# Which projections run beside which attention, and latents that stay on the chip

## The chip, the cores and the metric

The kernel runs on one core of a Trainium2 chip. A core has a matrix engine (TensorE, PE in the profile; its weight loads are listed apart as PEld), VectorE (DVE), ScalarE (ACT), GpSimd (POOL) and SyncE (SP), whose queue issues nearly all transfers here; 16 DMA engines move the data. The metric is the device time of one execution in microseconds. All arithmetic is float32; a product is made of three passes over operands that are split into a high and a low part (`fp32r` in the profile).

## What is computed

The reference is an encoder of two layers over 1024 positions of 1024 features. In each layer one input projection feeds four groups of attention heads (A to D), whose outputs are joined, projected and added; an MLP follows. The change concerns the input projection and its consumers:

```
h = rms_norm(x, norm1_g[l])
proj = h @ w_in[l]
(a_cq, a_ckv, a_kr, b_q, b_k, b_v, c_q, c_k, c_v, d_q, d_k, d_v) = split(proj)
y_a = mla_mixer(a_cq, a_ckv, a_kr, ...)   # group A: latents
y_b = diff_mixer(b_q, b_k, b_v, ...)      # group B
y_c = swa_mixer(c_q, c_k, c_v, ...)       # group C: a window of 128
y_d = na_mixer(d_q, d_k, d_v, ...)        # group D: neighbours on a grid
```

and inside group A the second projections, which start from the latents:

```
q = (rms_norm(cq, q_norm_g) @ w_uq)       # cq: 192 wide; rope on 32 of each head's 96
c = rms_norm(ckv, kv_norm_g)              # ckv: 128 wide
k_nope, v = c @ w_uk, c @ w_uv
k_pe = apply_rope(kr)                     # 32 wide, shared by the heads
```

## The kernel before

Everything is held with features on the partitions and positions along the row. The input projection has 19 column tiles of 128. Each is 8 blocks of 128 x 128 weights against both halves (512 positions) of the normed x, three passes each: 48 matmuls. The normed x (`xs`, high and low) fills all 16 places of the pool of big tiles. The projection is taken on x times the gain, and the row factor of the norm (`rb`) is multiplied in when a tile is evacuated.

`attention` (line 377) goes through these stages in each layer. Two waves make the six tiles of group B. Then `weave` (line 541) interleaves a main stream with a fill stream: after each step of attention it takes some steps of a list of projections. Beside B's attention (`attn_b`, 18 steps) the fill is `proj_latent` (line 661, three tiles: cq, the rest of cq with the rotary key kr, and ckv) and then `proj_d` (six tiles). Beside D's attention (`attn_d`, line 1030, 36 steps) the fill is `proj_c` (four tiles) and then `latent_up` (line 692, the seven second projections of group A). Then come the attentions of C and A with parts of the output projection as fill, then the MLP. Small chains that finish the softmax and the norms (`tails`, advanced by `tick`) run in between.

The order of instructions on each engine is chosen by a planner when the program is built: it starts from the program's order and priorities (the main stream has an offset, `LB` 40 and `LD` 50) and a model of times. So fill work of B may still run when D begins. A tile of a pool waits until an earlier one of its tag is free.

The places that matter:

- `stack` (line 737): 8 places of 128 x 1024 (the pool that holds x between stages). A head of B takes four (two q, two k), one of D three, one of A four.
- big tiles: 16 places; `xs` until the last input projection, then `rq`, `rkv` (the two row factors of the latents' norms, spread over the partitions) and six `latp` (high and low of three latents), and later the mixed outputs.
- `part` (line 571): 3 places of 128 x 512 for an evacuated half; `both` (line 574): 2 places for its high and low.
- The rotary tables `tabc`, `tabs` (`table`, line 561): one place each. They are loaded and multiplied with the row factor: for B with `rb` on VectorE, for C with `rb` on GpSimd, for the latents' second projection with `rq` on GpSimd.

In `proj_latent` each half of a tile is evacuated (times `rb`, line 603), squared on ScalarE, summed over the partitions by four matmuls against ones (line 655), multiplied by the gain, split, and written to a DRAM tensor `lat` (`latent_parts`, line 647, and `emit_parts`, line 578). After the third tile two reciprocal roots (`rsqrt_cols`, line 241: eleven operations on eight columns) give the two row factors, which are transposed and written to DRAM (`rows_of`, line 266). `latent_up` spreads them over the partitions by a broadcasting load (`spread`, line 281), loads `lat` back into `latp`, the second tile of cq twice (64 rows, above and below, so that a product over 64 rows can take two weights at a time), and multiplies. The rope of a tile (`ev_rope`, line 586) is three VectorE operations, one addition on `self.eng` (GpSimd here), and the split, whose low part is also on GpSimd.

Of the kernel before, what the change touches and what calls it, by code (L numbers as in the profile page):

```python
# [98 lines left out]
def layout(i):  # L99
# [29 lines left out]
    gq = np.concatenate([i["mla_q_norm_g"], np.zeros((n, 64), np.float32)], 1)  # L129
# [16 lines left out]
class Trunk:  # L146
# [107 lines left out]
    def rstd_cols(self, sq, count, rhs, tag="mm"):  # L254
# [5 lines left out]
        for t in range(n):  # L260
            nc.tensor.matmul(ps[:, t * g:(t + 1) * g], sq[:, t * P:(t + 1) * P], rhs, start=True, stop=True)
# [115 lines left out]
    def attention(self, l):  # L377
# [11 lines left out]
        lat, krd = dr([2, 3, P, S], "lat"), dr([2, 16, 2, S], "krd")  # L389
# [30 lines left out]
        with ExitStack() as stack, ExitStack() as att:  # L420
            self.ap = att.enter_context(sbuf("att"))
            with self.banks(mm=2, tr=2, sb=3, pv=1):
                with sbuf("proj", "right") as self.pp:
# [32 lines left out]
                    fill = chain(self.proj_latent(l, one, xs, rb, tabs, lat, krd, rows), proj_d())  # L456
# [3 lines left out]
                    fill = chain(proj_c(), self.latent_up(l, lat, rows, qa, ka, va))  # L460
# [100 lines left out]
    def table(self, name, rb, eng):  # L561

        out = []
        for n in "cs":
            t = self.pp.tile([P, S], F, tag="tab" + n, bufs=1, name="tab" + n)
            self.load(t, self.d[n + name])
            self.tt(t, t, rb, eng=eng)
# [92 lines left out]

    def proj_latent(self, l, one, xs, rb, tabs, lat, krd, rows_out):
# [4 lines left out]
        for i, t, g in ((0, T_CQ, self.gq[:, l, 0:1]), (2, T_CKV, self.gkv[:, l:l + 1])):  # L666
            yield from one(t, xs, self.ev_plain(rb, lambda n, y: self.latent_parts(y, g, P, n, lat[:, i], squares[i])))
        c, s = tabs

        def ev(n, ps):  # L670
            sl = slice(n * 512, n * 512 + 512)
            y, t2 = self.part(), self.part()
            self.tt(y[0:64], ps[0:64], rb[0:64, sl])
            self.tt(y[64:112], ps[64:112], c[64:112, sl])
# [816 lines left out]
```

## Time and profile before

| What | Value |
|---|---|
| Three runs, median (lowest to highest) | 2729.45 us (2723.23 to 2731.46) |
| The profiled execution, time / span | 2728.97 / 2727.2 us |
| Mean granted TensorE clock | 0.967 |
| First softmax minimum of B (line 806), layer 0 / layer 1 | 88.1 / 1434.6 us |
| DMA traffic | 389.20 MB, mean 143 GB/s |

The profile is that of one execution. Views used below: the page (shares of each engine, the chain of work that ended last), the busy times of each engine in chosen stretches with the granted clock and the use of the DMA engines, the instructions in order of time with the idle time before each and what ended it, groups of instructions of one line and shape, and the list of transfers.

### The profile page before, as it was taken

What the parts mean: (1) busy time and instruction counts of PE and PEld (TensorE: products, weight loads), DVE (VectorE), ACT (ScalarE), POOL (GpSimd) and SP (SyncE); (2) the same over time, 40 slices, a digit from 0 to 9 for tenths busy, and PEclk for the clock granted to TensorE, in tenths of its full rate; (3) what the DMA queues carried; (4) which work ended last, traced back from release to release, by engine and by line L of the source; (5) the groups of instructions that cost most, each with busy time, mean ns of one, the idle gap of its engine ahead of it and who ended that gap; (6) DMA issues with size and microseconds to landing.
All of it is one profiled execution on the core that took longest, in us unless ns stands there. A gap on an engine that the chain in (4) does not pass through costs nothing.

```text
span 2727.2 us, 37613 instructions
## 1 busy us (share of the span) xinstructions
PE 2553.1 (94%) x12298; PEld 2110.1 (77%) x12298; DVE 1994.1 (73%) x3544; ACT 1430.9 (52%) x2547; POOL 1134.5 (42%) x754
## 2 busy tenths in 40 slices
PE   8989988899989999999999899889998999999997
PEld 6778876787778887888877688767886788878886
DVE  7787767674966669787567778677749666687786
ACT  4667757563534444444436676576635344444444
POOL 2555642111245554445435556331013455545552
PEclk9989999999989999999998899899999999999998
DMA  5534597231234447444244345972221444664431
GB/s 175 166 105 126 154 280 241 83 93 40 65 130 156 151 160 267 156 138 142 98 133 138 95 134 157 300 215 71 76 70 44 154 159 149 223 222 150 131 100 62
DMA packets 190516, 389.20 MB, mean 143 GB/s; under 512 B 23712, under 2 KB 30832, under 8 KB 190320
## 3 DMA queue, kind: packets, MB, share of 16 engines
q1 hardware_dynamic: 176496, 361.62, 43.0%
q10 hardware_dynamic: 13824, 25.17, 2.7%
q8 instruction: 98, 1.61, 0.3%
q14 instruction: 98, 0.80, 0.1%
HBM read 263.29 MB, written 123.41 MB: 142 GB/s over the span
## 4 chain that ended last, share of the span: by engine, by line
PE 70%; DVE 14%; DMA 7%; ACT 4%; issue 3%; SPq 1%; POOL 1%; DVEq 0%; ACTq 0%; POOLq 0%
PE u L220 8%; PE u L222 8%; PE u L221 8%; PE mm L220 5%; PE mm L221 5%; PE mm L222 5%; PE p L220 5%; PE p L221 5%; PE p L222 5%; PE sb L804 3%; PE tr L840 2%; DVE p L806 2%; DVE part L188 2%; PE pv L829 2%; PE pv L828 2%
## 5 line engine op out<-in xcount | busy, mean ns | idle before, releaser
L188 POOL TENSOR_TENSOR wl<-raw,wh 128x512 fp32r<-128x512 f32 x448 | 635.1, 1418 | 705.2 <-ACT wh L194 690.1
L194 ACT ACTIVATE wh<-raw 128x512 fp32r<-128x512 f32 x448 | 281.5, 629 | 579.8 <-PE u L221 315.0
L188 POOL TENSOR_TENSOR wl<-ws,wh 128x512 fp32r<-128x512 f32 (+1 forms) x112 | 148.1, 1325 | 456.9 <-ACT wh L194 426.0
L220 PE MATMUL u<-far,wh 128*128 128x512 f32 x768 | 301.5, 393 | 11.5 <-ACT ev L1237 8.3
L188 DVE TENSOR_TENSOR raw<-raw 128x512 f32<-128x512 f32 x256 | 226.4, 890 | 107.4 <-POOL wl L188 56.9
L222 PE MATMUL u<-far,wl 128*128 128x512 f32 x768 | 300.5, 391 | 1.9 <-POOL wl L188 1.9
L221 PE MATMUL u<-far,wh 128*128 128x512 f32 x768 | 300.3, 391 | 0.0
L188 DVE TENSOR_TENSOR ptl<-tr,pth 128x512 fp32r<-128x512 f32 (+2 forms) x384 | 238.3, 628 | 66.6 <-ACT pth L194 64.9
L809 ACT ACTIVATE p<-p,nm 128x1024 f32<-128x1024 f32 x192 | 220.1, 1147 | 99.8 <-DVE nm L806 98.9
L194 ACT ACTIVATE pth<-tr 128x512 fp32r<-128x512 f32 (+2 forms) x384 | 205.6, 546 | 121.0 <-PE tr L840 64.8
L220 PE MATMUL p<-far,wh 128*128 128x512 f32 x640 | 251.7, 393 | 7.6 <-DVE ev L188 7.6
L222 PE MATMUL p<-far,wl 128*128 128x512 f32 x640 | 250.9, 392 | 1.5 <-POOL wl L188 1.5
L221 PE MATMUL p<-far,wh 128*128 128x512 f32 x640 | 251.0, 392 | 0.0
L804 PE MATMUL sb<-stack 96*128 96x512 f32 x640 | 218.5, 424 | 24.7 <-DVE nm L806 24.0
L188 DVE TENSOR_TENSOR far<-act,far 128x512 fp32r<-128x512 f32 x224 | 208.6, 960 | 14.6 <-ACT far L194 14.6
L188 POOL TENSOR_TENSOR p<-p 128x1024 f32<-128x1024 f32 x64 | 154.3, 2415 | 141.1 <-ACT p L893 125.0
L220 PEld LDWEIGHTS u<-far,wh 128*128 128x128 f32 x768 | 145.4, 189 | 43.6 <-ACT ev L1237 9.2
L222 PEld LDWEIGHTS u<-far,wl 128*128 128x128 f32 x768 | 145.0, 189 | 33.2 <-POOL wl L188 2.7
L220 PE MATMUL mm<-xh,wh 128*128 128x512 f32 x416 | 169.4, 407 | 0.8 <-DVE rows L272 0.2
L806 DVE CUSTOM_DVE_ANT_0 p<-sb,zero,nm 128x512 f32<-128x512 f32 x192 | 142.4, 743 | 36.3 <-PE sb L804 32.8
L221 PEld LDWEIGHTS u<-far,wh 128*128 128x128 f32 x768 | 145.3, 189 | 30.2
L221 PE MATMUL mm<-xl,wh 128*128 128x512 f32 x416 | 166.6, 400 | 0.0
(243 smaller groups left out, 6147.0 us busy)
## 6 DMA issues: line engine op xcount, KB each, us to landing
act<-acts SPq DMA_DIRECT2D x224, 256.0 KB
raw<-in_w_up SPq DMA_DIRECT2D x128, 256.0 KB
acts<-ev SPq DMA_DIRECT2D x128, 256.0 KB
raw<-in_w_down SPq DMA_DIRECT2D x128, 256.0 KB
acts<-ev ACTq DMA_DIRECT2D x96, 256.0 KB
ws<-in_w_in SPq DMA_DIRECT2D x76, 256.0 KB
rz<-drows SPq DMA_DIRECT2D x40, 256.0 KB
stack<-kd SPq DMA_DIRECT2D x32, 256.0 KB
```

The costliest lines, as they stand in the source:

```text
L188: (eng or self.nc.vector).tensor_tensor(out=out, in0=a, in1=b, op=op)
L194: nc.scalar.activation(hi, src, AF.Copy)
L220: mm(ps, w[0], x[0][:, sl], start=start, stop=False)
L221: mm(ps, w[0], x[1][:, sl], start=False, stop=False)
L222: mm(ps, w[1], x[0][:, sl], start=False, stop=stop)
L804: self.nc.tensor.matmul(ps, q[:, qt * P:(qt + 1) * P], k[:, sl], start=i == 0, stop=i == len(passes) - 1)
L806: self.nc.vector.tensor_tensor_reduce(out=p[:, sl], in0=ps, in1=self.zero[:, 0:1].bitcast(F).broadcast_to([P, 512]), scale=-scale, scalar= ...
L809: self.nc.scalar.activation(p, p, AF.Exp, bias=nm[:, 1:2], scale=-1.0, accum_out=z)
L828: nc.tensor.matmul(out, v[:, kt], h[:, sl], start=kt == 0, stop=False)
L829: nc.tensor.matmul(out, v[:, kt], lo[:, sl], start=False, stop=kt == 7)
L840: nc.tensor.transpose(t[:, k * 256 + i * P:k * 256 + (i + 1) * P], p[:, (j * 2 + k) * P:(j * 2 + k + 1) * P], self.ident)
```

## The change

Beside B's attention now run `proj_d` and then `proj_c`; beside D's attention run `proj_latent` and then `latent_up`. The three latents are evacuated into float32 tiles of the `stack` kind, 128 x 1024, and stay there; after the third tile they are multiplied by the gain and split into `latp` without leaving the chip. `lat` in DRAM is gone. The second tile of cq is written twice, to partitions 0 to 63 and 64 to 127, so its squares count double and are weighted with 0.5, and its gain is doubled in the constants (a column of the same length). The rotary key is multiplied by `rb` first and then rotated with bare tables, which are loaded in `proj_latent`, kept, and multiplied with `rq` in `latent_up`. The reciprocal root of cq is issued before the third tile. `rstd_cols` writes its sums group by group, so that `spread` reads one contiguous row.

```
-    gq = np.concatenate([i["mla_q_norm_g"], np.zeros((n, 64), np.float32)], 1)
+    gq = np.concatenate([i["mla_q_norm_g"], i["mla_q_norm_g"][:, 128:192]], 1)
...
-            nc.tensor.matmul(ps[:, t * g:(t + 1) * g], sq[:, t * P:(t + 1) * P], rhs, start=True, stop=True)
+            nc.tensor.matmul(ps.rearrange("p (g t) -> p t g", g=g)[:, t], sq[:, t * P:(t + 1) * P], rhs,
+                             start=True, stop=True)
...
-        src = rows.rearrange("(t g) p -> g t p", g=g)[j]
-        n = dst.shape[0]
-        self.load(dst.rearrange("p (t q) -> p t q", t=8), src.partition_broadcast(n))
+        src = rows.rearrange("(g t) p -> g (t p)", g=g)[j]
+        self.load(dst, src.partition_broadcast(dst.shape[0]))
...
-                    fill = chain(self.proj_latent(l, one, xs, rb, tabs, lat, krd, rows), proj_d())
+                    fill = chain(proj_d(), proj_c())
                     self.weave(chain.from_iterable(self.attn_b(l, t, qb, kb, vb, y["b"]) for t in range(2)),
                                fill, self.RB, self.LB, every=self.EV[0])
                     self.tails.append(self.mix_b(mix, y["b"], self.gsub[:, l:l + 1]))
-                    fill = chain(proj_c(), self.latent_up(l, lat, rows, qa, ka, va))
+                    lat = []
+                    fill = chain(self.proj_latent(l, one, xs, rb, lat, krd, rows),
+                                 self.latent_up(l, lat, rows, qa, ka, va))
                     self.weave(self.attn_d(l, qd, kd, vd, y["d"]), fill, self.RD, self.LD, every=self.EV[1])
...
-    def latent_parts(self, y, g, rows, n, dst, squares):
+    def latent_squares(self, y, n, squares):
         nc = self.nc
-        sl = slice(n * 512, n * 512 + 512)
         sq = self.part()
-        nc.scalar.activation(sq[:rows], y[:rows], AF.Square)
+        nc.scalar.activation(sq, y, AF.Square)
         ps = self.bank("mm", [P, 4])
         for t in range(4):
-            nc.tensor.matmul(ps[:, t:t + 1], sq[:rows, t * P:(t + 1) * P], self.ones[:rows, 0:1],
-                             start=True, stop=True)
+            nc.tensor.matmul(ps[:, t:t + 1], sq[:, t * P:(t + 1) * P], self.ones[:, 0:1], start=True, stop=True)
         nc.vector.tensor_copy(squares[:, n * 4:n * 4 + 4], ps)
-        self.emit_parts(y[:rows], [(dst[:, :rows, sl].rearrange("a p s -> p a s"), slice(0, rows))],
-                        slice(0, rows), g[:rows])
...
+        y = [self.stack(F) for _ in range(3)]
+        c, s = self.tabs = self.table("32")
+
+        def plain(i):
+            def ev(n, ps):
+                sl = slice(n * 512, n * 512 + 512)
+                self.tt(y[i][:, sl], ps, rb[:, sl])
+                self.latent_squares(y[i][:, sl], n, squares[i])
+            return ev
...
+            for at in (0, 64):
+                self.tt(y[1][at:at + 64, sl], ps[0:64], rb[0:64, sl])
+            k, t, t2 = self.part(), self.part(), self.part()
+            self.tt(k[64:112], ps[64:112], rb[64:112, sl])
+            self.tt(t[64:112], k[64:112], c[64:112, sl])
+            self.tt(t2[64:80], k[96:112], s[96:112, sl])
+            self.tt(t2[96:112], k[64:80], s[64:80, sl])
+            self.tt(t[64:80], t[64:80], t2[64:80], ALU.add, self.eng)
+            self.tt(t[96:112], t[96:112], t2[96:112], ALU.subtract, self.eng)
...
+        yield from one(T_CQ, xs, plain(0))
+        yield from one(T_CQR, xs, ev)
+        q = squares[0]
+        nc.vector.scalar_tensor_tensor(out=q, in0=squares[1], scalar=0.5, in1=q, op0=ALU.mult, op1=ALU.add)
+        rms(q, 192)
+        yield from one(T_CKV, xs, plain(2))
+        rms(squares[2], 128)
+        for t, g in zip(y, (self.gq[:, l, 0:1], self.gq[:, l, 1:2], self.gkv[:, l:l + 1])):
+            h, lo = self.big_tile(R, "latp"), self.big_tile(R, "latp")
+            for sl in self.halves():
+                self.split(h[:, sl], lo[:, sl], t[:, sl], g)
+            lat.append((h, lo))
...
-        parts = []
-        for i, r in ((0, P), (1, 64), (2, P)):
-            p = []
-            for j in range(2):
-                t = self.big_tile(R, "latp")
-                for at in range(0, P, r):
-                    self.load(t.bitcast(F)[at:at + r], lat[j, i, :r])
-                p.append(t)
-            parts.append(tuple(p))
-        tabs = self.table("32", rq, nc.gpsimd)
+        for t in self.tabs:
+            self.tt(t, t, rq, eng=nc.gpsimd)
```

More of the change, by code (lines that the diff above doesn't have):

```diff
@@ L681, in ev, with rms @@
                 for h in range(2)], slice(64, 112))
[L682 to L687 removed]
+            self.latent_squares(y[1][:, sl], n, squares[1])
+        def rms(m, count):
             nc.vector.tensor_scalar(m, m, 1.0 / count, EPS, ALU.mult, ALU.add)
             rows_out.append(self.rows_of(self.rsqrt_cols(m)))
+        yield from one(T_CQ, xs, plain(0))
@@ L690, in proj_latent, with latent_up @@
         yield True
-    def latent_up(self, l, lat, rows, qa, ka, va):
+    def latent_up(self, l, parts, rows, qa, ka, va):
         nc, d = self.nc, self.d
@@ L724, in latent_up @@
         w0 = self.weights(d["w_lat"][l, 0])
-        yield from two([w0[0], both(w0[1])], parts[0:2], self.ev_rope(tabs, qr))
+        yield from two([w0[0], both(w0[1])], parts[0:2], self.ev_rope(self.tabs, qr))
         plain = lambda r, dst: self.ev_plain(r, self.to_parts(dst))
```

26 lines of the change are left out of this document (6 added, 20 removed).

## The prediction

> **What bounds the kernel now.** I read the page first, then the busy times by stretch, then the chain of waits and the instructions of the stretches that stood out.
>
> ```profile
> span 2727.2 us, 37613 instructions
> PE 2553.1 (94%) x12298; PEld 2110.1 (77%) x12298; DVE 1994.1 (73%) x3544; ACT 1430.9 (52%) x2547; POOL 1134.5 (42%) x754
> PE 70%; DVE 14%; DMA 7%; ACT 4%; issue 3%; SPq 1%; POOL 1%; DVEq 0%; ACTq 0%; POOLq 0%
> ```
>
> TensorE is the bound: 2553.1 of 2727.2 us, 70% of the chain that ended last. The change adds no product and takes none away, so it can win only idle TensorE time, or time in which TensorE ran below full clock. The next view is of stretches of the two attention layers; the columns are TensorE, weight loads, VectorE, ScalarE, GpSimd, each with its count, then the granted clock, the DMA share and GB/s.
>
> ```profile
> 150.00:190.00 40.00, 30.02 (x138) 23.74 (x137) 34.58 (x88) 24.54 (x38) 22.82 (x12) 0.79 0.29 80
> 190.00:340.00 150.00, 149.61 (x827) 127.90 (x826) 115.98 (x305) 112.28 (x182) 88.57 (x52) 1.00 0.48 136
> 340.00:420.00 80.00, 66.10 (x363) 55.78 (x361) 50.68 (x131) 45.32 (x114) 30.92 (x21) 0.94 0.99 284
> 360.00:390.00 30.00, 22.40 (x117) 19.43 (x117) 17.25 (x42) 13.82 (x33) 14.29 (x9) 0.89 1.02 294
> 390.00:500.00 110.00, 87.45 (x451) 67.51 (x450) 79.47 (x210) 70.74 (x179) 28.89 (x18) 0.91 0.70 217
> 1500.00:1540.00 40.00, 29.62 (x126) 22.05 (x125) 33.34 (x84) 23.26 (x37) 23.96 (x14) 0.74 0.28 80
> 1540.00:1690.00 150.00, 148.63 (x821) 125.53 (x820) 120.06 (x298) 109.14 (x175) 85.32 (x49) 1.00 0.45 129
> 1720.00:1740.00 20.00, 13.56 (x65) 11.74 (x64) 12.06 (x33) 8.22 (x21) 9.84 (x7) 0.83 1.04 282
> 1740.00:1850.00 110.00, 93.25 (x489) 75.68 (x488) 82.44 (x219) 73.86 (x186) 30.72 (x19) 0.91 0.76 227
> ```
>
> Three kinds of stretch repeat in both layers. At 150 and 1500, where the last of the three latent tiles is worked on beside group B, VectorE is at 34.58 of 40 us and TensorE loses 10 us and a fifth of its clock. From 190 and 1540 TensorE is full. From 340 to 420 the DMA engines are full (0.99), and TensorE loses time until about 500. I count a loss as idle time plus busy time times (1 - clock).
>
> What happens in the first kind, from the order in time of GpSimd, VectorE and TensorE:
>
> ```profile
> 165.72 2.33 POOL L188 TENSOR_TENSOR tabs<-tabs,rb 128x1024 f32<-128x1024 f32 x1
> 168.12 2.34 DVE L249 SCALAR_TENSOR_TENSOR rs_t<-rs_r 128x8 f32<-128x8 f32 x2
> 173.63 0.80 PE L804 MATMUL sb<-stack 96*128 96x512 f32 x1 [4.98 <-DVE nm L806]
> 174.92 0.23 DVE L249 SCALAR_TENSOR_TENSOR rs_t<-rs_r 128x8 f32<-128x8 f32 x2
> ```
>
> The two reciprocal roots of `proj_latent` (line 689) are chains of eight-column operations. Two of them take 0.23 us at 174.92 but 2.34 us at 168.12, while GpSimd multiplies group C's rotary table and a softmax tile. The softmax minimum (line 806) queues behind them, and TensorE waits 4.98 us for it. In the second kind the chain of waits runs through transfers:
>
> ```profile
> 358.15 7.51 DMA rkv<-drows
> 365.69 11.75 DMA latp<-lat
> 399.02 5.40 DMA bias<-in_bias
> 404.43 9.07 DMA stack<-kc
> 413.57 9.20 DMA kan<-both
> 1713.22 10.30 DMA latp<-lat
> 1723.60 11.52 DMA stack<-kd
> ```
>
> `latent_up` needs eight free big tiles, and the normed x holds all sixteen until the last input projection; only then are scales and latents read back, 19.3 us in layer 0.
>
> **The change part by part.** *Order of the thirteen tiles beside B and D.* Each is 48 matmuls.
>
> ```profile
> 357.53 0.40 PE L222 MATMUL mm<-xh,wl 128*128 128x512 f32 x1
> ...
> 360.95 0.39 PE L222 MATMUL mm<-xh,wl 128*128 128x512 f32 x1
> ...
> 363.36 0.39 PE L222 MATMUL mm<-xh,wl 128*128 128x512 f32 x1
> ```
>
> Between the first two starts lie fifteen steps (the third is the last of the thirteen tiles): 3.42 / 15 = 0.228 us, so a tile costs 10.9 us of TensorE. B's fill gets one tile more (six of D and four of C for three latent and six), D's one less: plus 10.9 us where TensorE is full and minus 10.9 us later, in each layer. I cost this at **0**: up to the end of the thirteenth tile it is the same work in another order, and proj_c already overlaps B's end: its stores and B's last transposes (line 840) stand side by side.
>
> ```profile
> 313.80 13.16 SPq L167 DMA_DIRECT2D qc<-both  x6
> 353.51 0.44 PE tr L840 x4
> 424.64 0.39 DVE p L1084
> ```
>
> If D's start gives nothing back, it costs up to 2 x 10.9 = 21.9 us.
>
> *The burst at B's start.* It leaves with `proj_latent`, and proj_d's evacuations, simpler, come first. Loss now: 9.98 + 30.02 x 0.21 = 16.3 us in layer 0, 10.38 + 29.62 x 0.26 = 18.1 us in layer 1; together 34.4. The reciprocal roots and evacuations do not vanish; they go to D's start, where VectorE has 150 - 115.98 = 34 us of spare time, but the softmax behind them is as exposed. They no longer stand beside the multiplication by group C's table, though the one for `rq` may take its place. Between 0 and -34.4 I take half: **-17**.
>
> The Trainium skill's page "TensorE: Matmul & The Clock Gate" (Part 1: The HAM clock gate) says the clock halves after an idle window of about 3.4 us and returns after a busy one. The 4.98 us gap and the clock of 0.79 agree in kind; by the page one gap per layer would give back an estimated 1.7 us of clock, and the half would be about -12 instead of -17.
>
> *Latents on the chip.* What no longer moves, from the list of DMA issues:
>
> ```profile
> lat<-both SPq DMA_DIRECT2D x8, 512.0 KB
> latp<-lat SPq DMA_DIRECT2D x8, 512.0 KB
> kc<-both SPq DMA_DIRECT2D x8, 256.0 KB
> vc<-both SPq DMA_DIRECT2D x4, 512.0 KB
> latp<-lat SPq DMA_DIRECT2D x8, 256.0 KB
> lat<-both SPq DMA_DIRECT2D x4, 256.0 KB
> ```
>
> Per layer 4 x 512 + 4 x 256 KB = 3 MB of loads go, and 2.5 MB of stores. SP issues 14 DMAs fewer per layer. The loss at the read-back is 7.60 + 22.40 x 0.11 = 10.1 us in layer 0 and 6.44 + 13.56 x 0.17 = 8.7 in layer 1. The scales `rq` and `rkv` still go through DRAM (7.51 us) and still wait for big tiles; of the wait only 11.75 of 19.26 us is the latents': 0.61 x 18.8 = **-11.5**, between 0 and -18.8. The new hand-over, a split from SBUF straight into the freed tiles, has the same six halves as the old `emit_parts`, at another time.
>
> *Less traffic in the full stretch.* From 340 to 420 us some 284 GB/s x 80 us = 22.7 MB move. The 3 MB of latents and the 2 MB of kc and vc, which now go out beside B, are 22% of that. Ahead of group C the chain waits 23.7 us for bias, kc and kan. The losses from 390 to 500 and from 1740 to 1850 hold 22.55 + 16.75 = 39.3 us of idleness; 22% of it is **-8.6**, between 0 and twice that.
>
> *Added VectorE work.* `proj_latent` writes the half tile of cq twice and multiplies k by rb first.
>
> ```profile
> L188 DVE TENSOR_TENSOR part<-mm,rb 128x512 f32<-128x512 f32 x12 | 8.2, 686 | 0.8 <-PE mm L222 0.8
> L198 DVE SCALAR_TENSOR_TENSOR both<-part,par,both 128x512 fp32r<-128x512 f32 x8 | 8.7, 1092 | 1.2 <-ACT both L197 1.2
> ```
>
> That is two operations more per half, 2 x 2 x 2 x 0.686 = 5.5 us in all; VectorE's spare time covers most: **+2** of 0 to 5.5.
>
> *Places.* Three latents in float32 take three of the eight `stack` places until they are split. A head of D takes three, so one head's last keys can't be fetched until its forerunner is done. Such a load stood 11.52 us on the chain at 1723.60. Two heads per layer could be hit: 0 to 46 us. Some 33 us of latent tiles cover TensorE meanwhile, so I take **+5**. If that cover is used up, the whole wait shows, and the late thing next is C's first head, whose loads stand behind D's on SP's queue.
>
> *Nothing:* the contiguous spread, the group-first order of `rstd_cols`, the doubled gain and the factor 0.5 change forms, not counts; they are hidden under TensorE's full stretches, and uncovered they are below one eight-column operation each.
>
> Sum: -17 - 11.5 - 8.6 + 2 + 5 = -30 us. The profiled execution took 2728.97 us around its span of 2727.2, against a median of 2729.45: forecast **2699 us**, 2674 to 2716 if this case holds.
>
> **The rivals.** *All of it* (chance 0.10): burst and latents' losses vanish whole: -34.4 - 18.8 - 8.6 + 2 = -60, 2669 us. For it: both losses stand in both layers. Against: the reciprocal roots remain.
>
> *The burst only moves* (0.16): at D's start it costs what it cost at B's. -11.5 - 8.6 + 2 + 5 = -13, 2716 us. For it: the work is the same and VectorE stays in order.
>
> *GpSimd beside B* (0.12). The evacuations of C's rotary tiles put two GpSimd operations on each of six halves per layer next to B's softmax.
>
> ```profile
> L188 POOL TENSOR_TENSOR both<-part,both 128x512 fp32r<-128x512 f32 x48 | 64.8, 1354 | 60.3 <-ACT both L194 51.8 <-DMA ws<-in_w_out 4.1 <-PE mm L270 2.7
> L188 POOL TENSOR_TENSOR part<-part 128x512 f32<-128x512 f32 x24 | 32.9, 1369 | 20.7 <-DVE part L188 17.7 <-PE tr L221 1.3 <-PE tr L222 1.3
> ```
>
> Six times (1.354 + 1.369) is 16.3 us a layer, 33 in all. If each held up a VectorE operation for its whole length and TensorE with it, the gain of about 30 would be eaten: 2729 us, no change. Against it: such operations already run near 340 us with TensorE full, and VectorE at 115.98 + 16.3 of 150 would still fit. The Trainium skill's page "SBUF — State Buffer" (SBUF: two separate sides) has the rule behind this: VectorE with two SBUF inputs and GpSimd take one shared port pair in turn, and the loser blocks for the whole instruction. The 2.34 against 0.23 us above agrees.
>
> *The places decide* (0.22), on the other side: the three latents hold the `stack` places, D's heads run one after another behind their loads, and D's end, not TensorE, sets when C and A start. From the point where the wait is longer than the 33 us of latent tiles it shows in full: +46 + 5.5 - 17 - 11.5 = +23, 2752 us. For it: the pool was full with two heads of B, and D's loads are on the chain. Against: the latents are split right behind the last tile.
>
> *It doesn't do what it says* is kept inside these: if the planner spread proj_c past B's end as it does now, the latents would come after 363 us with their roots uncovered, which is the burst rival or worse.
>
> **How the numbers follow.** The forecast has 0.40. Runs before spread over 8 us, 0.3%, which is about what can be told from no change here. Faster by more: 0.40 + 0.10 + most of the burst rival, 0.62. Within: the GpSimd rival, 0.12. Slower: places and the worse ends, 0.26. The range runs from the full gain, 2667, to short of the places' price, 2746, which leaves out some 0.06 below and 0.13 above.
>
> **What would show it.** The slice at B's start (150 to 190) should have TensorE near 1.00 clock and no wait over 2 us behind line 806; the latents' names gone from the chain; the idle stretch after the last input tile shorter than 7.6 us; the stretch to C's end with less than 22 us idle. Wrong would be: reciprocal roots of 2 us and TensorE waiting behind them at D's start, `stack<-kd` on the chain for tens of us, C's first scores (line 1084, here 424.64 us) later than before. The prediction as a whole is wrong if TensorE's idle time in attention doesn't fall.

## The result, and the profile after

| Kernel | Median | Against before (95% interval) | Span of the profiled execution |
|---|---|---|---|
| before | 2729.83 us | | 2727.2 us |
| after | 2760.14 us (2759.86 to 2761.17, 4 runs) | 1.0116 (1.0099 to 1.0134) | 2758.0 us |

The change makes the kernel about 31 us slower; 2699 was forecast, with 2746 as the upper end. Of the experiments below, scales_ready and fill_faster each had one execution of four that was far longer (4800.74 and 7433.23 us), which is left out of their medians and ratios. Head of the page after:

```profile
span 2758.0 us, 37539 instructions
PE 2569.0 (93%) x12298; PEld 2119.4 (77%) x12298; DVE 1996.7 (72%) x3552; ACT 1432.7 (52%) x2547; POOL 1138.7 (41%) x754
```

The products are the same 12298, but they took 2569.0 us in place of 2553.1, at a mean granted clock of 0.962 in place of 0.967, and there is more idleness besides. To see where, each attention layer is cut into five stretches at points of its own trace: from B's first score 100 us on, then to the last input projection (377.5 us in layer 0 of after), to the last second projection, to the end of C's softmax, and to the end of A's scores. First the kernel before, with the columns as in the prediction (stretch, its length, TensorE, weight loads, VectorE, ScalarE, GpSimd, clock, DMA share, GB/s):

```profile
83.00:183.00 100.00, 84.81 (x406) 68.30 (x405) 85.47 (x203) 68.25 (x110) 57.76 (x33) 0.86 0.46 134
183.00:363.00 180.00, 179.38 (x993) 153.46 (x993) 132.11 (x347) 128.97 (x220) 98.48 (x57) 1.00 0.53 149
363.00:438.00 75.00, 59.11 (x322) 48.74 (x321) 55.91 (x141) 47.01 (x121) 25.98 (x17) 0.93 0.95 287
438.00:479.00 41.00, 34.55 (x182) 26.39 (x182) 29.67 (x94) 29.00 (x78) 9.78 (x6) 0.92 0.65 199
479.00:624.00 145.00, 132.72 (x788) 112.51 (x787) 107.19 (x241) 87.63 (x154) 21.53 (x12) 0.96 0.27 81
1431.00:1531.00 100.00, 84.93 (x390) 67.42 (x389) 82.23 (x195) 65.20 (x104) 56.62 (x32) 0.81 0.44 127
1531.00:1717.00 186.00, 184.40 (x1010) 156.15 (x1009) 139.86 (x354) 130.67 (x225) 98.81 (x59) 1.00 0.51 146
1717.00:1786.00 69.00, 55.90 (x298) 47.08 (x297) 50.78 (x129) 42.47 (x105) 25.40 (x17) 0.88 0.99 295
1786.00:1840.00 54.00, 44.56 (x229) 35.54 (x229) 40.37 (x115) 37.31 (x96) 18.16 (x10) 0.91 0.67 195
1840.00:1969.00 129.00, 123.26 (x761) 106.09 (x760) 98.36 (x230) 83.27 (x150) 12.81 (x8) 1.00 0.27 79
```

And the same view of the kernel after:

```profile
85.00:185.00 100.00, 90.31 (x443) 73.77 (x443) 71.52 (x174) 65.26 (x104) 56.09 (x31) 0.93 0.47 147
185.00:377.00 192.00, 180.49 (x975) 152.25 (x974) 147.62 (x366) 133.39 (x224) 101.00 (x59) 0.95 0.40 112
377.50:450.00 72.50, 55.68 (x254) 44.79 (x253) 50.93 (x134) 38.72 (x99) 24.64 (x16) 0.79 0.87 250
450.00:513.00 63.00, 51.03 (x262) 40.73 (x261) 43.58 (x125) 40.78 (x105) 18.12 (x10) 0.89 0.60 173
513.00:641.00 128.00, 122.17 (x750) 104.63 (x749) 97.54 (x228) 82.36 (x147) 12.81 (x8) 1.00 0.29 80
1447.00:1547.00 100.00, 92.99 (x464) 76.27 (x463) 75.40 (x180) 66.48 (x106) 54.34 (x31) 0.95 0.46 145
1547.00:1736.00 189.00, 177.29 (x958) 148.62 (x957) 144.97 (x360) 130.97 (x221) 100.79 (x59) 0.96 0.41 112
1736.00:1808.00 72.00, 53.85 (x253) 41.96 (x252) 48.39 (x132) 38.52 (x98) 25.00 (x17) 0.81 0.89 250
1808.00:1874.00 66.00, 53.65 (x262) 41.14 (x262) 46.53 (x126) 41.58 (x106) 18.13 (x10) 0.87 0.56 168
1874.00:2001.00 127.00, 121.87 (x753) 105.04 (x751) 97.60 (x226) 82.30 (x147) 12.80 (x8) 1.00 0.28 80
```

The loss of a row is its idle time plus busy time times (1 - clock), as in the prediction. The first row of before gives 15.19 + 84.81 x 0.14 = 27.1 us, that of after 9.69 + 90.31 x 0.07 = 16.0. The table adds both layers and takes the last two stretches together; four of the experiments below stand beside them, worked out alike:

| Loss of TensorE, both layers, us | before | after | order_only | copy_scalar | light_all | one_copy |
|---|---|---|---|---|---|---|
| first 100 us of B | 58.3 | 27.7 | 26.0 | 24.0 | 25.5 | 47.4 |
| then to the last input projection | 2.2 | 39.3 | 38.6 | 36.9 | 25.0 | 8.8 |
| then to the last second projection | 39.8 | 56.9 | 82.2 | 51.1 | 39.2 | 36.5 |
| then to the end of A's scores | 46.0 | 47.9 | 44.6 | 39.8 | 40.0 | 40.7 |
| sum | 146.3 | 171.8 | 191.5 | 151.8 | 129.7 | 133.4 |
| sum against before | | +25.5 | +45.2 | +5.5 | -16.6 | -12.9 |
| span against before | | +30.8 | +49.9 | +3.8 | -16.2 | -13.0 |

The last two lines agree within 5.3 us in every column, so the time is in these stretches. The burst at B's start did shrink, by 30.6 us, but 37.1 us came back by the end of the input projection, and another 17.1 by the end of the second projections. Idle time alone rose from 95.4 to 110.2 us over the ten stretches; the prediction had named idle time that doesn't fall as the sign that it is wrong as a whole.

What took its place stands at D's start. VectorE in order of time there, and the ten microseconds around it, in the kernel after:

```profile
380.00:390.00 10.00, 5.99 (x40) 4.98 (x38) 9.83 (x30) 6.63 (x21) 4.70 (x2) 0.97 1.04 279
```

```profile
380.74 0.73 DVE L198 SCALAR_TENSOR_TENSOR latp<-stack,par,latp 128x512 fp32r<-128x512 f32 x1
...
383.93 2.10 DVE L249 SCALAR_TENSOR_TENSOR rs_t<-rs_r 128x8 f32<-128x8 f32 x1
...
386.43 1.94 DVE L188 TENSOR_TENSOR rs_t<-rs_t,sq 128x8 f32<-128x8 f32 x1
...
389.40 0.17 DVE L188 TENSOR_TENSOR rs_t<-rs_t,sq 128x8 f32<-128x8 f32 x1
```

VectorE makes the low parts of the latents, a head's softmax and a reciprocal root in the same ten microseconds, one after another: it is busy for 9.83 of them, TensorE for 5.99. Two eight-column steps take 2.10 and 1.94 us where the same kind takes 0.17 a little later. GpSimd does at that time what the prediction named as a possible successor, the products of the rotary tables with `rq`:

```profile
383.64 2.37 POOL L188 TENSOR_TENSOR tabc<-tabc,rq 128x1024 f32<-128x1024 f32 x1 [3.91 <-DMA rq<-drows]
385.97 2.37 POOL L188 TENSOR_TENSOR tabs<-tabs,rq 128x1024 f32<-128x1024 f32 x1
```

The Trainium skill's page "SBUF — State Buffer" (SBUF: two separate sides) has a VectorE operation with two SBUF inputs and a GpSimd operation take a shared port pair in turn. These two pairs agree with it, as the pair of before did: each VectorE step ends within 0.03 us of the GpSimd product beside it.

TensorE's own order shows how far the second projections have moved away from the last input projection, after:

```profile
377.54 0.39 PE L222 MATMUL mm<-xh,wl 128*128 128x512 f32 x1
391.49 0.78 PE L220 MATMUL mm<-latp,wh 128*128 128x512 f32 x1
```

and before, where 363.36 us was the last input projection:

```profile
366.98 0.50 PE L220 MATMUL mm<-latp,wh 128*128 128x512 f32 x1 [1.33 <-DMA latp<-lat]
```

From the last input tile to the first second projection it is 14 us instead of 3.6; in between TensorE works on D's heads and stands idle for 4.4 us. Later, in group C, ScalarE and VectorE in order of time after:

```profile
427.72 0.51 ACT L1097 ACTIVATE p<-p,nb 128x256 f32<-128x256 f32 x1 [1.45 <-DVE nb L1094]
...
435.13 0.60 ACT L645 ACTIVATE both<-mm 128x512 fp32r<-128x512 f32 x1 [5.59 <-DMA kan<-both]
...
445.89 0.61 DVE L1094 CUSTOM_DVE_ANT_0 p<-sb,mask,nsink 128x384 f32<-128x384 f32 x1
...
448.00 0.61 ACT L1097 ACTIVATE p<-p,nb 128x384 f32<-128x384 f32 x1
```

The second projections' results wait for one of the two `both` places to be stored, and C's softmax stands behind them: it started at 427.72, its next minimum on VectorE (line 1094) comes at 445.89 and its next exponential on ScalarE (line 1097) at 448.00, some 20 us later.

### The profile page after: what moved, and what is told of

It reads as the page before. It is cut to its first block, busy times and chain, and to the rows that moved or that the text cites. A ratio compares the mean times of both kernels' runs of the same rounds, so it can differ in the third digit from the quotient of the medians.

```text
span 2758.0 us, 37539 instructions
## 1 busy us (share of the span) xinstructions
PE 2569.0 (93%) x12298; PEld 2119.4 (77%) x12298; DVE 1996.7 (72%) x3552; ACT 1432.7 (52%) x2547; POOL 1138.7 (41%) x754
## 2 busy tenths in 40 slices
DMA packets 182386, 377.64 MB, mean 137 GB/s; under 512 B 23264, under 2 KB 26288, under 8 KB 182192
## 4 chain that ended last, share of the span: by engine, by line
PE 68%; DVE 14%; DMA 6%; ACT 4%; issue 4%; POOL 2%; SPq 0%; DVEq 0%; ACTq 0%; POOLq 0%
PE u L220 8%; PE u L222 8%; PE u L221 7%; PE p L220 5%; PE p L221 5%; PE p L222 5%; PE mm L220 5%; PE mm L221 5%; PE mm L222 4%; PE sb L814 3%; DVE p L816 3%; DVE part L188 2%; PE tr L850 2%; DVE ptl L188 1%; PE pv L839 1%
## 5 line engine op out<-in xcount | busy, mean ns | idle before, releaser
L814 PE MATMUL sb<-stack 96*128 96x512 f32 x640 | 215.7, 418 | 13.1 <-DVE nm L816 12.2
L850 PE MATMUL tr<-ident,p 128*128 128x128 f32 x1024 | 159.9, 275 | 9.9 <-DVE ptl L188 6.0
```

The source lines that it names most:

```text
L814: self.nc.tensor.matmul(ps, q[:, qt * P:(qt + 1) * P], k[:, sl], start=i == 0, stop=i == len(passes) - 1)
L850: nc.tensor.transpose(t[:, k * 256 + i * P:k * 256 + (i + 1) * P], p[:, (j * 2 + k) * P:(j * 2 + k + 1) * P], self.ident)
```

## The experiments

Ratios are to the kernel before on the same chip, whose median in these batches was 2726 to 2731 us. Theories: the order is what costs (latents last, their chain in the open); the `stack` places hold up D; VectorE's work at D's start is too much; the scales or the form of the spread.

**order_only.** The new order, with the latents still through DRAM and without the double write of the query's half tile (after to this):

```
+            self.emit_parts(y, [(lat[:, i, :r, sl].rearrange("a p s -> p a s"), slice(0, r))], slice(0, r),
+                            gains[i][:r])
...
-            for at in (0, 64):
-                self.tt(y[1][at:at + 64, sl], ps[0:64], rb[0:64, sl])
+            self.tt(k[0:64], ps[0:64], rb[0:64, sl])
...
+                    self.load(t.bitcast(F)[at:at + r], lat[j, i, :r])
```

> The changed order of the projections, but the latents go through DRAM as before (no latent holds a stack place; the cq tile isn't written twice, so two VectorE operations per half of that tile are gone as well). Theory P (places: the three latents in the stack pool delay the loads of D's second head): about the time before, 2715 to 2735 us, and D's second head scores within 10 us of the first. Theory O (order: the latents' evacuations, squares and roots beside D's start, and latent_up later, cost the time wherever the latents lie): about the time after, 2750 to 2765 us, with TensorE idle around the last latent tile.

Measured: 2776.59 us, 1.0170 (1.0148 to 1.0193), beyond both ranges. Of the two VectorE operations that the expectation counts as gone, the edit takes out one, the second write. When the latents pass through DRAM the order costs 46 us (the key's multiplication ahead of its rotation and the shared tables are in it too). The stretch from the last input projection to the last second one in each layer, and of layer 0 the chain of waits:

```profile
380.00:456.00 76.00, 49.31 (x236) 38.23 (x235) 45.97 (x112) 33.13 (x78) 25.52 (x17) 0.80 0.81 236
1751.00:1832.00 81.00, 51.98 (x206) 37.08 (x206) 45.55 (x100) 30.02 (x68) 25.17 (x17) 0.68 0.73 209
```

```profile
388.25 7.64 DMA bias<-in_bias
...
405.03 8.53 DMA latp<-lat
413.69 0.78 PE mm L741
```

The latents now come last, so their way out to DRAM and back is open: TensorE loses 82.2 us there, against 39.8 before. D's first two heads start at 336 and 354 us, as early as before (337 and 355), so this loss is not in D's places.

**places_held.** Before, with three `stack` tiles written before proj_c and read after it:

```
+                        held = [self.stack(F) for _ in range(3)]
+                        for t in held:
+                            nc.gpsimd.memset(t[:, 0:2], 0.0)
                         yield from proj_c()
+                        for t in held:
+                            nc.scalar.activation(t[:, 0:2], t[:, 0:2], AF.Copy)
```

> The kernel before, with three stack places taken from the start of D's fill until group C's projections are done (three small writes, three small reads). Theory P: 2750 to 2765 us, D's second head late by 20 to 30 us as in the changed kernel. Theory O: the time before, 2722 to 2738 us.

Measured: 2727.65 us, 0.9997 (0.9985 to 1.0009). It proves nothing, since the reads stand far ahead of proj_c's end in the planner's order. GpSimd's first write of a place, and ScalarE's read of it:

```profile
270.66 0.10 POOL L463 MEMSET stack<- 128x2 f32 x1
```

```profile
272.35 0.19 ACT L466 ACTIVATE stack<-stack 128x2 f32<-128x2 f32 x1
```

**d_first** and **spread_only.** Before, with D's projections ahead of the latents beside B, and before with only the new form of the spread:

```
-  fill = chain(self.proj_latent(l, one, xs, rb, tabs, lat, krd, rows), proj_d())
+  fill = chain(proj_d(), self.proj_latent(l, one, xs, rb, tabs, lat, krd, rows))
```

> The kernel before with the fill beside B turned round: D's projections first, then the latents' (still before group C's, still through DRAM). Theory P says nothing of it but no loss: 2715 to 2735 us. Theory O: the burst of latent work moves from B's start to the middle of B, where TensorE has B's whole stream beside it, and latent_up isn't delayed: 2710 to 2730 us. If the burst costs the same wherever it stands, 2727 to 2733.

> The kernel before with the contiguous spread and the group-first order of the sums alone. Both theories: no change that can be told, 2722 to 2735 us.

Measured: 2725.68 us, 0.9989 (0.9978 to 1.0001), and 2729.45 us, 1.0000 (0.9988 to 1.0012). Neither is a cause. With D first the latents leave B's start without a gain in time, which is what "the burst only moves" says. The first two stretches of layer 0 in d_first:

```profile
83.00:183.00 100.00, 98.09 (x506) 81.69 (x505) 78.61 (x195) 72.35 (x117) 55.53 (x33) 1.00 0.50 157
183.00:363.00 180.00, 165.33 (x909) 139.22 (x908) 142.61 (x363) 127.58 (x219) 100.64 (x57) 0.93 0.49 135
```

They lose 1.9 and 26.2 us, where before lost 27.1 and 0.6: the whole burst came back in the next stretch, without D's start or the new hand-over.

**scales_ready** and **fill_faster.** After, with the two row factors read from input tables that are there from the start (so the right scaling is left out); and after with a denser fill beside D (the ratio of steps to fill 1 to 2 rather than 3 to 2):

```
-        self.spread(rq, rows[0])
+        self.load(rq, d["c32"])
```

```
-    NP, RB, RD, LB, LD = 6, (7, 8), (3, 2), 40, 50
+    NP, RB, RD, LB, LD = 6, (7, 8), (1, 2), 40, 50
```

> The changed kernel with the two row factors of the latents' norms replaced by loads of input tables, which wait for no root (so group A's second projections are scaled wrongly; the roots and their transposes are still computed). If the chain root, transpose, DRAM, spread at the end of the latents is what delays latent_up and C: 2735 to 2748 us, the stretch from the last input tile to the last second projection shorter by 8 to 12 us in each layer. If the cost is the latents' evacuation beside D's start and the late end of the input tiles: 2752 to 2762 us.

> The changed kernel with two fill steps for each step of D instead of two for three: the latents come ahead of D's first heads in the program. If the loss is in the pace of the fill (latents and second projections too late for C): 2735 to 2750 us. If the latents' evacuation costs TensorE time wherever it stands at D's start: 2755 to 2770 us.

Measured: 2761.71 us, 1.0125 (1.0107 to 1.0142): the chain of scales isn't waited for. And 2792.63 us, 1.0239 (1.0222 to 1.0256), beyond both ranges: a denser fill beside D is worse. What it runs short of, the run doesn't show.

**one_copy** and **one_copy_d_first.** Before's order; each latent goes to DRAM once in float32, comes back into three `stack` places at the head of D's fill, and is split on the chip behind proj_c. The second has D's projections ahead of the latents:

```
-        self.emit_parts(y[:rows], [(dst[:, :rows, sl].rearrange("a p s -> p a s"), slice(0, rows))],
-                        slice(0, rows), g[:rows])
+        self.keep(dst[:rows, sl], y[:rows])
...
+                        y = [self.stack(F) for _ in range(3)]
...
+                                self.load(y[i][at:at + r], lat[i, :r])
+                        yield from proj_c()
...
+                                self.split(h[:, sl], lo[:, sl], t[:, sl], g)
```

> The order of the kernel before; the latents go through DRAM as one float32 copy, are loaded into three stack places at the start of D's fill and split on the chip once big tiles are free. If the part of the change that keeps latents out of the read-back is good in itself and only the order is bad: 2708 to 2722 us, with no wait for latents after the last input tile. If the read-back of the kernel before was hidden anyway: 2724 to 2734 us.

> The same with D's projections ahead of the latents' beside B: the sum of the two if they add, 2704 to 2720 us; no better than the one before if the loss at B's start only moves, 2708 to 2724.

Measured: 2716.69 us, 0.9963 (0.9950 to 0.9975), faster than both kernels; and 2728.99 us, 1.0007 (0.9992 to 1.0021), slower than either expectation: D's projections first cost 12 us here and nothing in d_first, and no run says why. In the table, one_copy gains most in the first 100 us of B (47.4 for 58.3), where the latents' splits no longer stand, and only 3.3 us up to the last second projection. In one_copy three places are in fact held while D begins, from the loads to the splits:

```profile
329.05 2.29 SPq L160 DMA_DIRECT2D stack<-lat  x3
```

```profile
354.81 0.71 ACT L197 ACTIVATE latp<-stack,par 128x512 fp32r<-128x512 f32 x1
```

D's first head starts at 336 us all the same, and the second at 356 (before 355). That the latents hold places is thus not enough to make the kernel slower.

**fill_slower.** After, with a thinner fill beside D:

```
-    NP, RB, RD, LB, LD = 6, (7, 8), (3, 2), 40, 50
+    NP, RB, RD, LB, LD = 6, (7, 8), (2, 1), 40, 50
```

> The changed kernel with one number altered: beside group D's heads the fill is drawn two parts to one step of attention instead of three to two. If the time is lost only because latents and second projections are drawn at the wrong pace (faster was 34 us worse), 2735 to 2745 us. If the loss is the latents' own chain at D's start (evacuation, squares, split, each in VectorE's order), the pace is no remedy: 2755 us or more. The share of the second projections' end in the loss should be seen in the time of the last latp matmul, 450.0 us in the changed kernel.

Measured: 2742.42 us, 1.0047 (1.0027 to 1.0068), some 19 us better than after and in the range given for the pace. But the last second projection still ends at 449.1 us (450.0), so the gain isn't that the second projections end earlier; C's softmax ends at 500 instead of 513.

**light_evac** and **light_all.** After, with lighter work for the latents; both make the first edit and leave out the row factor and the rotation of the key; light_all also makes the second, leaves out the roots and reads the row factors from tables:

```
-            for at in (0, 64):
-                self.tt(y[1][at:at + 64, sl], ps[0:64], rb[0:64, sl])
+            self.tt(y[1][0:64, sl], ps[0:64], rb[0:64, sl])
+            nc.scalar.activation(y[1][64:128, sl], y[1][0:64, sl], AF.Copy)
```

```
-                self.split(h[:, sl], lo[:, sl], t[:, sl], g)
+                nc.scalar.activation(h[:, sl], t[:, sl], AF.Copy, scale=g)
+                nc.scalar.activation(lo[:, sl], t[:, sl], AF.Copy, scale=g)
```

> The changed kernel with a lighter evacuation of the second latent tile: the rotation of the rotary key is left out (that key is wrong), and the upper copy of the query's half tile is made by ScalarE from the lower one, so per half four VectorE operations of about 0.7 us and two of GpSimd go, 8 and 4 in a layer. If VectorE's load at D's start sets the loss in proportion, 8 x 0.69 x 2 layers = 11 us come back: about 2749. If the loss is where the latents stand and not what they cost VectorE, 2757 to 2762, with the last input tile still about 14 us later than in the kernel before.

> As light_evac, and in addition the reciprocal roots with their row transposes are left out (scales come ready from input tables, so all scaling by them is wrong), and the low parts of the latents are made by a second ScalarE copy instead of VectorE's subtraction (the low part is wrong). Some 16 VectorE operations of a half tile and both chains of roots go in a layer. If VectorE's work for the latents at D's start is the cost, nearly the whole loss goes: 2725 to 2740. If it is that the second projections begin only when the last input tile is done and split, however light the work, it stays within 10 us of the changed kernel: 2750 to 2762. Between the two, both have a share, and the difference to light_evac is the share of roots and splits.

Measured: 2731.71 us, 1.0005 (0.9990 to 1.0020), and 2708.85 us, 0.9926 (0.9901 to 0.9950). Both beat what was expected of them: the operations taken out return more than their own time. In light_all the first second projection follows the last input one by 6 us, and the stretch of the second projections loses no more than before (39.2 us in both layers, 39.8 before).

**added_off, split_off, roots_off, better.** They part the gain of the last two: after without the two operations per half that the change adds (the first edit of light_evac and the one here); with the splits of light_all alone; without the roots alone (row factors from tables); and with relief by other engines (copy by ScalarE, low part by GpSimd, thinner fill).

```
-            self.tt(k[64:112], ps[64:112], rb[64:112, sl])
-            self.tt(t[64:112], k[64:112], c[64:112, sl])
+            self.tt(t[64:112], ps[64:112], c[64:112, sl])
```

```
-            rows_out.append(self.rows_of(self.rsqrt_cols(m)))
+            pass
```

```
-                self.split(h[:, sl], lo[:, sl], t[:, sl], g)
+                nc.scalar.activation(t[:, sl], t[:, sl], AF.Copy, scale=g)
+                self.split(h[:, sl], lo[:, sl], t[:, sl], None, nc.gpsimd)
```

> The changed kernel without the two operations per half that the change adds: the upper copy of the query's half tile is made by ScalarE, and the rotary key isn't multiplied by its row scale (left out, so the key is wrong); the rotation itself stays. Four VectorE operations of 0.69 us per layer go, 5.5 us of VectorE time in all. light_evac, which leaves out the rotation too (two more VectorE and two GpSimd operations per half), was 28 us faster than the changed kernel. If the added work is the larger part of it, 2738 to 2746; if the moved rotation with its GpSimd steps is, 2751 to 2758. By the prediction's own term, +2, it would be 2758.

> The changed kernel with the low parts of the latents made by a second ScalarE copy instead of VectorE's subtraction (the low part is wrong, the rest stands): six VectorE operations of 0.86 us per layer go, 10 us in all, of those between the last input tile and the second projections. light_all was 23 us faster than light_evac, by roots and splits together. If the split is the larger part, 2740 to 2748 here and roots_off above 2753; if the roots are, the other way round.

> The changed kernel with both reciprocal roots and their row transposes left out, and their scales read from input tables (all scaling by them is wrong): some 17 small VectorE operations each go from D's start, and the second projections no longer depend on them. scales_ready, which kept the roots but did not wait for them, was as slow as the changed kernel, so a gain here would be VectorE's time and not the wait: 2738 to 2748 if the roots are the larger part of the 23 us, above 2753 if the split is.

> Nothing is left out: the changed kernel with VectorE relieved where another engine can do the step, the upper copy of the query's half tile by ScalarE, the low part of each latent by GpSimd (which needs the gain applied by ScalarE first), and the fill beside D at two parts to one step. The slower fill alone gave 18 us, light_evac 28. If VectorE's load at D's start is the cause, 2720 to 2735, near the kernel before or under it. If GpSimd's longer subtraction (about 1.4 to 2 us a half) only takes the place of VectorE's in the chain from the last input tile to the second projections, 2735 to 2745, no better than the slower fill alone.

| | Median | Ratio (95%) |
|---|---|---|
| added_off | 2731.79 us | 1.0020 (1.0008 to 1.0031) |
| split_off | 2746.66 us | 1.0075 (1.0055 to 1.0096) |
| roots_off | 2746.38 us | 1.0070 (1.0054 to 1.0087) |
| better | 2741.42 us | 1.0052 (1.0037 to 1.0066) |

Against after's 1.0116 the added work is worth 0.96%, 26 us, the splits and the roots 11 and 13 us, about half each, which neither expectation had. With light_evac's 1.11% the three make 1.98%, near light_all's 1.90%, so these three gains add. In better they don't: it is no better than the thinner fill alone.

**copy_scalar, mended, mended_slower.** After with only the upper copy of the half tile moved to ScalarE (the diff under light_evac); with the key's multiplication by `rb` taken off VectorE too, by tables multiplied on GpSimd and loaded again for the second projections; and this with the thinner fill.

```
-        c, s = self.tabs = self.table("32")
+        c, s = self.table("32", rb, nc.gpsimd)
...
-        for t in self.tabs:
-            self.tt(t, t, rq, eng=nc.gpsimd)
+        tabs = self.table("32", rq, nc.gpsimd)
```

> Nothing is left out: the changed kernel with the upper copy of the query's half tile made by ScalarE; the key's multiplication by its row scale stays on VectorE. added_off, without both added steps, gave back 28 us. If the double write is the larger part, 2732 to 2742; if the key's multiplication, which stands ahead of the rotation and takes a third scratch tile, is, 2750 to 2760.

> Nothing is left out: both added steps taken off VectorE. ScalarE makes the upper copy, and the rotary tables are multiplied by the row scale on GpSimd and loaded again for the second projections, as in the kernel before. If added_off showed the price of the added VectorE work and not of the missing key scale, 2728 to 2738. If GpSimd's two table products (2.3 us each beside D's softmax) and the second loading cost what they cost beside B, 2740 or more.

> As mended, with the fill beside D at two parts to one step. If the slower fill's 18 us and the added work's 28 us are separate losses, 2710 to 2722, under the kernel before. If both act through the same thing, VectorE's load per us at D's start, 2725 to 2738, no better than mended.

Measured: 2733.23 us, 1.0006 (0.9994 to 1.0019); 2743.83 us, 1.0047 (1.0029 to 1.0065); 2738.77 us, 1.0029 (1.0018 to 1.0040). With nothing else changed, one line decides nearly all of the loss: with the double write off VectorE the kernel takes the time of before. This is what it is in the kernel after, per half, on VectorE:

```profile
347.37 1.38 DVE L188 TENSOR_TENSOR stack<-mm,rb 64x512 f32<-64x512 f32 x2 [0.57 <-PE mm L222]
```

and in copy_scalar on ScalarE, beside half of it on VectorE:

```profile
343.35 0.63 ACT L679 ACTIVATE stack<-stack 64x512 f32<-64x512 f32 x1 [0.28 <-DVE stack L188]
```

That is 0.69 us of VectorE's time per half, 1.4 us per layer, and it returns about 15 us per layer. It does not return at the place itself: of the 20.0 us that copy_scalar's table column is smaller than after's, 6.1 come up to the last input projection and 13.9 behind it. In layer 0 the two double writes stand at 326.17 and 347.37 us. The ten microseconds around each, in the kernel after:

```profile
325.00:335.00 10.00, 6.51 (x37) 5.41 (x37) 9.25 (x21) 6.23 (x13) 5.36 (x3) 0.82 0.00 0
345.00:355.00 10.00, 7.30 (x52) 6.54 (x51) 8.00 (x17) 6.32 (x15) 4.13 (x3) 1.00 0.23 69
```

In copy_scalar the same two stretches have VectorE at 8.93 and 8.99 us and TensorE at 7.40 and 6.95, so they are no emptier there.

mended does less on VectorE than copy_scalar and is 11 us slower, by GpSimd's table products, the second loading, or another order: it does not tell which. better has copy_scalar's edit too and is 0.46% slower, by GpSimd's subtraction, the gain on ScalarE or the thinner fill. And the thinner fill, worth 19 us on after, is worth some 5 on mended, with intervals that overlap, so these gains don't add. So a few microseconds of work move the result by ten and more here, and part of that may be that the planner writes another order for every engine when an edit changes its modelled times; no run holds the order fixed. How much of the double write's price is VectorE's time and how much the order that came with it stays open.

## Why the prediction was wrong

The miss of 61 us falls into two parts of about the same size. copy_scalar is the changed kernel without the double write. By the prediction's terms it should have been some 31 us faster than before, and it was 2 us slower (1.0006): 33 us lie in the order, the burst, the hand-over, the traffic and the places together. The double write brought 30 where about 1 was put down for it. By its own terms:

- **Order of the thirteen tiles, 0.** This is the first step that failed: +46 us when the latents go through DRAM (order_only); with the latents on the chip its price alone wasn't measured. "Up to the end of the thirteenth tile it is the same work in another order" holds for the tiles and leaves out what hangs on them. Before, the latents came first and had some 190 us until they were needed (roots at 168, read back from 358 us); C's tiles, which came last, were not needed until C. Now those with the longest successors come last: evacuation, squares, roots, split and second projections stand behind one another, at D's start, when VectorE is full.
- **The burst at B's start, -17.** The half was wrong in both directions. At its place 30.6 us went, close to the whole of 34.4, and 37.1 came back by the last input projection; d_first shows the same without the rest of the change (25.2 us gone, 25.6 come back in layer 0). The rival "the burst only moves" had the mechanism right; its 2716 rested on the other terms. Its sign of recognition was the prediction's own: eight-column steps of 2 us at D's start. One reading in the term was off: the 2.34 us pair before didn't stand beside the product of C's table, which ended at 168.05 us, but beside the softmax tile's (from 168.02, 2.34 us).
- **Latents on the chip, -11.5.** The mechanism was right and its size too small for this order: from order_only to copy_scalar, which differ mainly by the way through DRAM, it is 1.64%, 45 us. But most of this pays back what the order had just laid open. Against before, the stretch to the last second projection went from 39.8 to 51.1 us in copy_scalar.
- **Less traffic, -8.6.** No gain from it can be seen. Traffic fell from 389.20 to 377.64 MB and the DMA share of that stretch from 0.95 and 0.99 to 0.87 and 0.89, while the stretch lost more. The term divided a loss by bytes, as if TensorE waited for their rate; no run takes bytes away without a wait, so the term itself stays unmeasured.
- **Added VectorE work, +2.** The second step that failed: 26 us (added_off), all of it by the double write (copy_scalar gives back 30). The text set the work against "VectorE's spare time" and let that cover most of it. Around the two double writes VectorE is at 9.25 and 8.00 of 10 us and TensorE at 6.51 and 7.30. That the missing spare time is the reason isn't shown, since copy_scalar is as full there.
- **Places, +5.** Not the cause, as far as the runs show. D's second head was late after (380 us, before 355). But copy_scalar holds the same places, has that head late too (373 us), ends D as early as before (last exponential at 414.3 us, before 414.9) and takes the time of before; order_only has the head on time and is slower; and one_copy holds three places and is faster. The prediction's sign, `stack<-kd` on the chain for tens of us, is absent: between 320 and 440 us no such load is on it. "The places decide" gave 2752, the rival nearest in time, with a mechanism that these runs speak against. A size for the term was not measured.
- **Nothing, for the spread:** right (spread_only 1.0000), and the scales' chain was not waited for (scales_ready).
- **GpSimd beside B:** small. Between 185 and 285 us, where C's rotary tiles stand, after loses 5 us in layer 0:

```profile
185.00:285.00 100.00, 96.65 (x530) 81.40 (x529) 84.11 (x205) 73.34 (x118) 62.39 (x37) 0.98 0.46 132
```

Put together, by ratios: the order +46, the latents on the chip -45, the double write +30 make +31. That this is what was measured follows from how it is added up, from before over order_only and copy_scalar to after, and is no test of the parts. The chances failed with the sum: 0.26 was given to slower, and nearly all of it for the places.

A version that beats both kernels keeps the old order and takes only the smaller hand-over: one_copy, 0.9963 (0.9950 to 0.9975).

## What to carry to other kernels

When independent pieces of work change places, compare what hangs on each, not only their lengths: whatever goes last has its whole chain in the open, so the piece with the longest chain behind it should not be the one. In the middle, as in d_first, it cost nothing here. Spare time over a long stretch says little about the microseconds in which work lands: beside D's start VectorE was busy for 9.83 of 10 us. And where a planner writes the order, an edit of one operation can move the time by ten times its length, so a part is priced by a run with and without it, and by more than one such pair.

## What the runs showed of the hardware

- The time of a VectorE operation on 512 columns didn't depend on the partitions: 64 took 0.69 us (1.38 for two, above), and 128 in the same trace:

```profile
369.39 0.69 DVE L188 TENSOR_TENSOR stack<-mm,rb 128x512 f32<-128x512 f32 x1 [3.87 <-PE mm L222]
```

  Writing a half tile twice thus cost VectorE as much as writing two whole ones.
- Where TensorE had more gaps, its granted clock was lower as well. In order_only, layer 1, it was idle for 29.0 of 81 us and the clock was 0.68; before, the like stretch had 13.1 of 69 us idle at 0.88. Matmuls of one shape in them (`mm<-latp,wl`, 128x512) took 562 ns on average and 400 before. In the kernel after, TensorE worked all ten microseconds from 335 to 345 us at a clock of 0.67, behind ten with 3.49 us idle; before it had 10.00 us there at 1.00, behind ten with 0.10 idle.
